# Recurrence of the first layer: products by chunk of 64 tokens and head in the array's four quarters, a PSUM bank to each row half, inverses joined to 64x64 blocks

## The chip, the cores and the metric

The kernel runs on one core of one Trainium2 chip. The metric is the device time in microseconds (us) of one execution, the median over runs. TensorE (PE in the rows; PEld is its weight load) multiplies, VectorE (DVE), ScalarE (ACT) and GpSimd (POOL) work element by element, SyncE (SP) issues the DMAs. Each engine runs its instructions in the order in which the program lists them.

## The reference, cut to what matters

Two residual layers on 512 tokens of width 1024. The first layer's mixer has two halves: sparse attention (8 heads of 64, the best 128 keys by an indexer) and RWKV-7 time mixing (8 heads of 64), a generalised delta rule that the change touches:

```
def step(state, inp):
    r_t, w_t, k_t, v_t, kk_t, a_t = inp
    sa = einsum('bhvk,bhk->bhv', state, -kk_t)
    state = state * w_t + sa[..., None] * (kk_t * a_t) + v_t[..., None] * k_t
    return state, einsum('bhvk,bhk->bhv', state, r_t)
_, y = lax.scan(step, state0, xs)          # 512 tokens, state 64x64 for each of 8 heads
y = head_norm(y) * gn_g + gn_b
y = (y + bonus) * g
```

Then come an output projection, a feed-forward block and a gated embedding; the second layer (mLSTM) and a second feed-forward block follow. All of it is float32.

## The kernel before, in words

Activations lie with features on the 128 partitions and the 512 tokens along the free dimension. `project` makes the large products: each float32 weight is split into a high and a low part, and three matmuls (lines 212 to 214) of 128x128 by 128x512 are added in PSUM. These are most of the program.

The recurrence (`rwkv`) is brought into chunk form. The 512 tokens are eight chunks of 64, handled two at a time: `c` runs over four pairs of 128 tokens, `i` over the two chunks of a pair, which lie on the two row halves of a token-major tile. Heads lie in pairs too: head h = 2j+g is on row half g of feature tile j. For each pair of chunks:

- `r_in` makes the strictly lower products of the keys (`pair_products`, line 719, masked on DVE), turns tiles to token-major (`tokens`, line 833) and makes the right side z = [W | U].
- `corner` (for two pairs at once) builds 32x32 blocks of the inverse of the unit triangular matrices, with the off-diagonal 32x32 block in a tile `off`. `expand` (lines 823 to 827) spreads these on POOL into a 128x128 block-diagonal matrix per head, and `r_apply` (line 916) multiplies it with z.
- `r_read` makes the products of the queries with both keys (`pair_products` again, four calls), and line 928 masks each on DVE and widens it to a 128x128 matrix per head, whose other chunk's block is zero.
- `r_step` makes q (line 944), then for each chunk G and H (bank "gh", lines 958, 960, 963), and carries the state over (line 975, then lines 978 to 980 on DVE). For a chunk G and H are products of rows of one row half.
- `r_out` makes the output y: two products over all 128 rows (lines 1009 and 1011) and one with the state (line 1016), head pair after head pair, then squares, group norm and gate.

A matmul of 64 rows and 64 columns uses one quarter of the array (rows 0-63 or 64-127, columns 0-63 or 64-127). A float32 matmul stands in the trace as two records, each with its weight load.

PSUM has eight banks: four are `aux` (handed out in turn, and taken again only when the engine that reads the bank is done), three are "mm", one is "po". `take` and `give` hand out SBUF slots in turn.

The order of the instructions follows from `merge` in `rwkv`: the part `front(c)` of the next pair of chunks, `back(c-1)` of the last one, the attention (`attend`, then `mixes`, the output projection's first half) and the embedding's projection (`embed`) are generators that are stepped in fixed ratios, one `yield` at a time; the framework's scheduler then shifts instructions a little. So PE's list interleaves the recurrence with attention and with projections.

Of the kernel before, what the change touches and what calls it, by code (L numbers as in the profile page):

```python
# [18 lines left out]
P = 128  # L19
# [30 lines left out]
class Trunk:  # L50
# [43 lines left out]
    def constants(self):  # L94
# [11 lines left out]
        self.mincl = cp.tile([P, P], F32, name="mincl")  # L106
        tri(self.mincl, OP.is_ge)
        nc.gpsimd.memset(self.mincl[0:64, 64:128], 0.0)
        work = self.take()
        tri(work[:, :P], OP.is_gt)  # L110
        self.mstrict = cp.tile([P, 64], F32, name="mstrict")
        for r in (slice(0, 64), slice(64, 128)):
            nc.gpsimd.tensor_copy(self.mstrict[r], work[r, r])
        self.give(work)

        self.mdiag = cp.tile([P, 4], F32, name="mdiag")
        nc.gpsimd.memset(self.mdiag, 0.0)
        for b in range(4):
            nc.gpsimd.memset(self.mdiag[32 * b:32 * b + 32, b:b + 1], 1.0)
# [591 lines left out]
    def pair_products(self, left, right, c, g):  # L711

        ps = self.aux("pair")
        r = slice(64 * g, 64 * g + 64)
        for j in range(4):

            for i in range(2):
                t = slice(P * c + 64 * i, P * c + 64 * i + 64)
                self.nc.tensor.matmul(ps[64 * i:64 * i + 64, tl(j, 64)], left[j][r, t], right[j][r, t],
                                      start=True, stop=True)  # L720
        return ps[:, :256].rearrange("p (j t) -> p j t", t=64)
# [5 lines left out]
    def pairs_ab(self):  # L727

        nc = self.nc
        self.raws = self.takes(NT, "raw")  # L730
        ab = self.dram.tile([P, 32 * 32], F32, name="ab")
        for c, raw in enumerate(self.raws):
            for g in range(2):
                nc.scalar.copy(self.parity(raw, g), self.pair_products(self.Bt, self.KK, c, g))
            r3 = raw.rearrange("s (h t) -> s h t", t=64)
            for b in range(4):
                p0 = b * 32 + c * 8
                nc.sync.dma_start(ab[p0:p0 + 8].rearrange("h (s t) -> s h t", t=32),
                                  r3[32 * b:32 * b + 32, :, 32 * (b % 2):32 * (b % 2) + 32])
        nc.sync.dma_start(self.big[1][:, :1024], ab)  # L740

    def solve(self):
# [21 lines left out]
        self.invs, self.offs = [None, None], [None, None]  # L764
        self.inv, self.off = [None] * NT, [None] * NT
        return last

    def corner(self, two):
# [24 lines left out]
        nc.vector.transpose(dt, inv)  # L793
        yield
# [13 lines left out]
        off = d  # L808
        nc.scalar.mul(off[0:32], ps[0:32], -1.0)
        nc.vector.tensor_scalar(off[64:96], ps[64:96], -1.0, None, op0=OP.mult)  # L810
        self.invs[two], self.offs[two] = inv, off
        for i in range(2):
            c = 2 * two + i
            self.inv[c], self.off[c] = (t[:, tl(i, 256)].rearrange("p (h t) -> p h t", t=32) for t in (inv, off))
        self.give(dt, f, *self.raws[2 * two:2 * two + 2])
        yield

    def expand(self, out, c, g):

        nc = self.nc  # L820
        o4 = out.rearrange("s (h b t) -> s h b t", b=4, t=32)
        h = slice(4 * g, 4 * g + 4)
        nc.gpsimd.tensor_tensor(o4, self.inv[c][:, h].unsqueeze(2).to_broadcast([P, 4, 4, 32]),
                                self.mdiag.unsqueeze(1).unsqueeze(3).to_broadcast([P, 4, 4, 32]), op=OP.mult)
        for b in (0, 2):
            r = slice(32 * b, 32 * b + 32)
            nc.gpsimd.tensor_copy(o4[r, :, b + 1], self.off[c][r, h])
# [50 lines left out]
    def r_in(self, c):  # L878
# [5 lines left out]
        for g in range(2):  # L884
            nc.vector.tensor_tensor(self.parity(ak, g), self.pair_products(self.Kt, self.KK, c, g),
                                    self.mstrict.unsqueeze(1).to_broadcast([P, 4, 64]), op=OP.mult)
            yield
# [19 lines left out]
    def r_apply(self, c):  # L907
        nc, r = self.nc, self.r[c]
        z, tt = r["z"], self.takes(2, "tt")
        r["X"] = self.takes(2)  # L910
        for g in range(2):
# [7 lines left out]
        self.give(*z, *tt)  # L919

    def r_read(self, c):
        r = self.r[c]
        Rt = [self.Rt[:, j] for j in range(4)]
        mask = self.mincl.rearrange("p (b t) -> p b t", t=64).unsqueeze(1).to_broadcast([P, 4, 2, 64])
        for name, left in (("rb", self.Bt), ("rk", self.Kt)):
            r[name] = self.takes(2)
            for g in range(2):
# [3 lines left out]
                yield  # L931
        if c == NT - 1:
            self.give(*self.KK, *self.Bt, *self.Kt, *self.invs, *self.offs)

    def r_step(self, c):
        nc, r = self.nc, self.r[c]
        Bk, Kk, V = r["B"], r["K"], self.V[c]
        head = lambda h: (h // 2, slice(64 * (h % 2), 64 * (h % 2) + 64))
        W, U = self.WU(c)

        ps = self.aux("q")
        for h in range(8):
            j, p = head(h)
            nc.tensor.matmul(ps[p, tl(j)], W(h), r["rb"][h % 2][:, tl(h // 2)], start=True, stop=True)
        r["q"] = q = self.take()
        nc.vector.tensor_tensor(q.rearrange("p (j t) -> p j t", t=P), ps.rearrange("p (j t) -> p j t", t=P),
                                self.Rt[:, :, tl(c)], op=OP.add)
        yield
        r["S"] = [self.state]
        for i in range(2):  # L950
            n = 2 * c + i
            k = slice(64 * i, 64 * i + 64)
            ps = self.aux("gh")
            for j in range(4):
                two = [(h, head(h)[1]) for h in (2 * j, 2 * j + 1)]
                o = slice(256 + 64 * j, 256 + 64 * j + 64)
                for h, p in two:
                    nc.tensor.matmul(ps[p, o], Bk[k, tl(h, 64)], U(h)[k], start=True, stop=False)
                for h, p in two:
                    nc.tensor.matmul(ps[p, o], Kk[k, tl(h, 64)], V[k, tl(h, 64)], start=False, stop=True)  # L960
                if n:
                    for h, p in two:
                        nc.tensor.matmul(ps[p, tl(j, 64)], W(h)[k], Bk[k, tl(h, 64)], start=True, stop=True)
            new = self.take()
            pl = self.PL[:, n].unsqueeze(2).to_broadcast([P, 4, 64])
            s3 = new[:, :256].rearrange("p (j v) -> p j v", v=64)
            if n:
                gh = self.take()
                nc.scalar.copy(gh, ps)
                yield  # L970
                ps = self.aux("step")
                state = self.state
                for h in range(8):
                    j, p = head(h)
                    nc.tensor.matmul(ps[p, tl(j, 64)], gh[p, tl(j, 64)], state[p, tl(j, 64)],
                                     start=True, stop=True)
                sh = gh[:, 256:]
                nc.vector.tensor_tensor(sh, sh, state[:, :256], op=OP.add)
                nc.vector.tensor_tensor(sh, sh, ps[:, :256], op=OP.add)
                nc.vector.tensor_tensor(s3, sh.rearrange("p (j v) -> p j v", v=64), pl, op=OP.mult)  # L980
                self.give(gh)
            else:
                nc.vector.tensor_tensor(s3, ps[:, 256:].rearrange("p (j v) -> p j v", v=64), pl, op=OP.mult)
# [3 lines left out]
        self.give(Bk, Kk)  # L987
# [6 lines left out]
    def r_out(self, c):  # L994
# [3 lines left out]
        rb, rk, q, states = r["rb"], r["rk"], r["q"], r["S"]  # L998
# [5 lines left out]
        ps = self.aux("y")  # L1004

        for j in range(4):
            two = [(h, slice(64 * (h % 2), 64 * (h % 2) + 64)) for h in (2 * j, 2 * j + 1)]
            for h, p in two:
                nc.tensor.matmul(ps[p, tl(j)], U(h), rb[h % 2][:, tl(j)], start=True, stop=False)
            for h, p in two:  # L1010
                nc.tensor.matmul(ps[p, tl(j)], self.V[c][:, tl(h, 64)], rk[h % 2][:, tl(j)], start=False, stop=False)
            for i in range(2):
                k = slice(P * j + 64 * i, P * j + 64 * i + 64)
                for h, p in two:
                    if states[i] is not None:
                        nc.tensor.matmul(ps[p, k], states[i][p, tl(j, 64)], q[p, k], start=False, stop=i == 1)
        y, sq = self.takes(2)
        y3 = y.rearrange("p (j t) -> p j t", t=P)
        nc.scalar.activation(sq, ps, AF.Square)
        nc.vector.tensor_tensor(y3, ps.rearrange("p (j t) -> p j t", t=P), self.gate[:, :, tl(c)], op=OP.mult)  # L1020
# [14 lines left out]
        self.give(y, sq, *rb, *rk, q, *r["X"], self.V[c], *(s for s in states[:2] if s is not None))  # L1035
# [519 lines left out]
```

## Time and profile before

| what | value |
|---|---|
| median of 3 runs | 1625.3 us (1624.97 to 1631.96) |
| the profiled execution, its own time | 1628.07 us |
| its span on the core | 1626.4 us |
| PE busy | 1563.8 us (96% of the span) |
| DVE, ACT, POOL busy | 947.5, 684.6, 311.9 us |

In a row of the busiest groups stands: line, engine, operation, output<-inputs, shapes, number of instructions | busy time (overlaps counted once), mean duration of one in ns | idle time of the engine before them and what ended it. A matmul's duration holds its way through the array, so neighbours overlap: what one costs is read from the distance of the starts. The recurrence lies between 195 and 350 us of the span.

### The profile page before, as it was taken

The page shows a single profiled execution, that of the slowest core. Times are in us where ns is not written, and L with a number is a line of the kernel's source. Part 1 is how long each engine was busy: PE and PEld are TensorE (multiplying, and loading weights), DVE is VectorE, ACT ScalarE, POOL GpSimd, SP SyncE. Part 2 cuts the span into 40 slices and gives each one's busy share as a digit, 9 for nine tenths or more (in the row PEclk, how much of TensorE's full clock was granted, in tenths as well). Part 3 has the DMA queues.
Part 4 walks back from the last instruction along what each step waited for, and adds up shares of the span by engine and source line. Part 5 has one row for each costly group of instructions (what it writes and reads, how often), then busy time and mean ns, then how long its engine had stood idle before and what let it go on. Part 6 is the DMA issues. An engine that isn't in the chain of part 4 may idle for free.

```text
span 1626.4 us, 24626 instructions
## 1 busy us (share of the span) xinstructions
PE 1563.8 (96%) x9446; PEld 1260.8 (78%) x9446; DVE 947.5 (58%) x1755; ACT 684.6 (42%) x1259; POOL 311.9 (19%) x292
## 2 busy tenths in 40 slices
PE   8889899999999999999999999999999999999998
PEld 5566668778888888888777777787778888888887
DVE  6979956666444444335676657566664444443345
ACT  5643465525333333324454555353453333333233
POOL 5545230212000000002400334352430000000002
PEclk9989999999999999999999999999999999999999
DMA  4124120113332333334322113121232333333332
GB/s 165 46 66 132 44 93 2 48 65 95 96 97 94 98 97 110 94 104 139 123 85 85 53 46 104 59 65 62 62 104 91 98 97 98 97 94 96 97 103 98
DMA packets 90110, 142.42 MB, mean 88 GB/s; under 512 B 19588, under 2 KB 24708, under 8 KB 89992
## 3 DMA queue, kind: packets, MB, share of 16 engines
q1 hardware_dynamic: 89992, 140.84, 28.1%
q8 instruction: 74, 1.21, 0.3%
q14 instruction: 44, 0.36, 0.1%
HBM read 133.26 MB, written 7.54 MB: 87 GB/s over the span
## 4 chain that ended last, share of the span: by engine, by line
PE 71%; DVE 6%; issue 1%; ACT 1%; POOL 1%; DMA 0%; DVEq 0%; POOLq 0%
PE mm L212 22%; PE mm L213 21%; PE mm L214 21%; PE v L1296 1%; PE S L1263 1%; PE S L1264 1%; PE num L1310 1%; PE S L1262 1%; PE num L1312 1%; PE num L1311 1%; POOL t L1425 1%; PE gates L1148 1%; DVE wlo L173 0%; DVE t L1342 0%; DVE t L1424 0%
## 5 line engine op out<-in xcount | busy, mean ns | idle before, releaser
L172 ACT CAST whi<-wraw 128x512 fp32r<-128x512 f32 (+1 forms) x470 | 283.9, 606 | 576.7 <-PE mm L213 519.8
L212 PE MATMUL mm<-x,whi 128*128 128x512 f32 (+1 forms) x1248 | 492.0, 394 | 3.3 <-ACT x L298 3.3
L214 PE MATMUL mm<-x,wlo 128*128 128x512 f32 (+1 forms) x1248 | 488.8, 392 | 3.4 <-POOL wlo L173 3.3
L213 PE MATMUL mm<-x,whi 128*128 128x512 f32 (+1 forms) x1248 | 488.3, 391 | 0.3 <-DVE x L299 0.3
L173 DVE TENSOR_TENSOR wlo<-wraw,whi 128x512 fp32r<-128x512 f32 x352 | 244.4, 695 | 247.3 <-ACT whi L172 246.7
L212 PEld LDWEIGHTS mm<-x,whi 128*128 128x128 f32 x1248 | 235.7, 189 | 56.8 <-ACT x L298 3.7
L214 PEld LDWEIGHTS mm<-x,wlo 128*128 128x128 f32 x1248 | 236.0, 189 | 53.7 <-POOL wlo L173 5.1
L213 PEld LDWEIGHTS mm<-x,whi 128*128 128x128 f32 x1248 | 236.0, 189 | 48.5 <-issue 1.2
L173 POOL TENSOR_TENSOR wlo<-wraw,whi 128x512 fp32r<-128x512 f32 (+1 forms) x118 | 154.4, 1314 | 317.1 <-ACT whi L172 309.5
L308 POOL TENSOR_TENSOR t<-t 128x512 f32<-128x512 f32 x42 | 56.7, 1351 | 764.2 <-ACT t L307 763.9
L212 PE MATMUL mm<-h,whi 128*128 128x512 f32 x352 | 136.9, 389 | 0.0
L213 PE MATMUL mm<-h,whi 128*128 128x512 f32 x352 | 136.9, 389 | 0.0
L214 PE MATMUL mm<-h,wlo 128*128 128x512 f32 x352 | 136.9, 389 | 0.0
L214 PEld LDWEIGHTS mm<-h,wlo 128*128 128x128 f32 x352 | 66.1, 188 | 13.8
L213 PEld LDWEIGHTS mm<-h,whi 128*128 128x128 f32 x352 | 66.1, 188 | 13.7
L212 PEld LDWEIGHTS mm<-h,whi 128*128 128x128 f32 x352 | 66.1, 188 | 13.7
L1371 DVE TENSOR_TENSOR t<-mm,t 128x512 f32<-128x512 f32 x44 | 30.4, 692 | 67.1 <-PE mm L214 67.1
L1369 DVE TENSOR_TENSOR t<-mm,t 128x512 f32<-128x512 f32 x44 | 30.4, 692 | 66.4 <-PE mm L214 64.8
L177 ACT CAST h<-t 128x512 fp32r<-128x512 f32 x44 | 27.3, 621 | 65.0 <-DVE t L1372 65.0
L212 PE MATMUL mm<-y,whi 128*128 128x512 f32 x128 | 51.4, 401 | 1.1 <-DVE t L1353 1.1
L213 PE MATMUL mm<-y,whi 128*128 128x512 f32 x128 | 51.5, 402 | 0.0
L214 PE MATMUL mm<-y,wlo 128*128 128x512 f32 x128 | 50.9, 397 | 0.0
(387 smaller groups left out, 2159.1 us busy)
## 6 DMA issues: line engine op xcount, KB each, us to landing
wraw<-in_ffn_w_gate_dram SPq DMA_DIRECT2D x88, 256.0 KB, 2.6
wraw<-in_ffn_w_up_dram SPq DMA_DIRECT2D x88, 256.0 KB, 2.6
wraw<-in_ffn_w_down_dram SPq DMA_DIRECT2D x80, 256.0 KB, 2.7
wraw<-in_c_w_up_dram SPq DMA_DIRECT2D x64, 256.0 KB, 2.6
wraw<-in_w_in_dram SPq DMA_DIRECT2D x38, 256.0 KB, 2.6
wraw<-in_ple_w_gate_dram SPq DMA_DIRECT2D x32, 256.0 KB, 2.7
wraw<-in_c_w_down_dram SPq DMA_DIRECT2D x32, 256.0 KB, 2.6
t<-in_x_dram SPq DMA_DIRECT2D x16, 256.0 KB, 3.0
```

The costliest lines, as they stand in the source:

```text
L172: nc.scalar.copy(hi, raw)
L173: self.wlo_engine.tensor_tensor(lo, raw, hi.bitcast(F32), op=OP.subtract)
L177: self.nc.scalar.copy(hi, src)
L212: nc.tensor.matmul(out, hi[:, c], xh, start=k == 0, stop=False)
L213: nc.tensor.matmul(out, hi[:, c], xl, start=False, stop=False)
L214: nc.tensor.matmul(out, lo[:, c], xh, start=False, stop=k == n - 1)
L308: nc.gpsimd.tensor_tensor(self.acc, self.acc, sq, op=OP.add)
L1148: nc.tensor.matmul(self.gps[32 * c:32 * c + 8, :P], self.maps[:, i, tl(w, 8)], src[:, tl(c)], start=False, stop=i == 15 and w == 1, tile_p ...
L1262: nc.tensor.matmul(ps[:, :n], xhi[i][:, c_], qhi[i][:, o:], start=i == 0, stop=False)
L1263: nc.tensor.matmul(ps[:, :n], xhi[i][:, c_], qlo[i][:, o:], start=False, stop=False)
L1369: nc.vector.tensor_tensor(gt, pg, self.rstd, op=OP.mult)
L1371: nc.vector.tensor_tensor(ut, pu, self.rstd, op=OP.mult)
```

## The change

Five things change, all in the recurrence. `pair_products` makes both heads of a pair in one go, into two banks, one for each row half, and walks through the four quarters of the array in turn; `r_read` makes the products with both keys in one call, and keeps 64x64 blocks where it widened them to 128. G and H of both chunks are made in one go in two banks, ahead of q; q and y go chunk by chunk, a bank to each chunk's row half. The output's state product is cut into pieces of 32 columns. `expand` is gone: `corner` writes the inverses as 64x64 blocks into a tile for each pair of chunks (POOL copies and zeros, then ACT and DVE the corner), and `r_apply` multiplies by quarter.

```
-    def pair_products(self, left, right, c, g):
-        ps = self.aux("pair")
-        r = slice(64 * g, 64 * g + 64)
-        for j in range(4):
-            for i in range(2):
-                t = slice(P * c + 64 * i, P * c + 64 * i + 64)
-                self.nc.tensor.matmul(ps[64 * i:64 * i + 64, tl(j, 64)], left[j][r, t], right[j][r, t],
+    def pair_products(self, lefts, right, c):
+        ps = [self.aux("pair") for _ in range(2)]
+        for l, left in enumerate(lefts):
+            for j in range(4):
+                o = slice(256 * l + 64 * j, 256 * l + 64 * j + 64)
+                for i in range(2):
+                    t = slice(P * c + 64 * i, P * c + 64 * i + 64)
+                    for g in range(2):
+                        r = slice(64 * g, 64 * g + 64)
+                        self.nc.tensor.matmul(ps[g][64 * i:64 * i + 64, o], left[j][r, t], right[j][r, t],
...
     def corner(self, two):
...
         nc.vector.transpose(dt, inv)
+        for i in range(2):
+            self.inv[2 * two + i] = whole = self.take("inv")
+            w4 = whole.rearrange("p (h b t) -> p h b t", h=8, t=32)
+            i4 = inv[:, tl(i, 256)].rearrange("p (h t) -> p h t", t=32)
+            for b in range(4):
+                s = slice(32 * b, 32 * b + 32)
+                nc.gpsimd.tensor_copy(w4[s, :, b % 2], i4[s])
+                if b % 2:
+                    nc.gpsimd.memset(w4[s, :, 0], 0.0)
...
-    def expand(self, out, c, g):
...
     def r_apply(self, c):
-        for g in range(2):
-            self.expand(tt[g], c, g)
...
-                nc.tensor.matmul(ps[:, tl(i)], tt[g][:, tl(i)], z[g][:, tl(i)], start=True, stop=True)
+                for k in (slice(0, 64), slice(64, 128)):
+                    nc.tensor.matmul(ps[k, tl(i)], inv[k, tl(4 * g + i, 64)], z[g][k, tl(i)], start=True, stop=True)
...
     def r_read(self, c):
-        for name, left in (("rb", self.Bt), ("rk", self.Kt)):
-            r[name] = self.takes(2)
-            for g in range(2):
-                self.nc.vector.tensor_tensor(
-                    r[name][g].rearrange("p (j b t) -> p j b t", b=2, t=64),
-                    self.pair_products(left, Rt, c, g).unsqueeze(2).to_broadcast([P, 4, 2, 64]), mask, op=OP.mult)
+        r["rbk"] = self.takes(2)
+        for t, ps in zip(r["rbk"], self.pair_products([self.Bt, self.Kt], Rt, c)):
+            self.nc.vector.tensor_tensor(t.rearrange("p (l j t) -> p l j t", j=4, t=64), ps, mask, op=OP.mult)
...
     def r_step(self, c):
+        ps = [self.aux("gh") for _ in range(2)]
+        each = [(i, k, h) for j in range(4) for i, k in enumerate(chunks) for h in (2 * j, 2 * j + 1)]
+        for n in range(0, 16, 4):
+            for left, right in ((Bk, None), (Kk, V)):
+                for i, k, h in each[n:n + 4]:
+                    j, p = head(h)
+                    nc.tensor.matmul(ps[i][p, 256 + 64 * j:320 + 64 * j], left[k, tl(h, 64)],
+                                     U(h)[k] if right is None else right[k, tl(h, 64)],
...
+        gh = self.takes(2)
+        for i in range(2):
+            o = 0 if c or i else 256
+            nc.scalar.copy(gh[i][:, o:], ps[i][:, o:])
+        yield
...
+        ps = [self.aux("q") for _ in range(2)]
+        for i, k, h in each:
             j, p = head(h)
-            nc.tensor.matmul(ps[p, tl(j)], W(h), r["rb"][h % 2][:, tl(h // 2)], start=True, stop=True)
+            nc.tensor.matmul(ps[i][p, tl(j, 64)], W(h)[k], rbk[h % 2][k, tl(j, 64)], start=True, stop=True)
...
     def r_out(self, c):
-        ps = self.aux("y")
+        ps = [self.aux("y") for _ in range(2)]
+        for l in range(2):
+            for j in range(4):
+                for i, k in enumerate(chunks):
+                    for h in (2 * j, 2 * j + 1):
+                        left = U(h)[k] if l == 0 else self.V[c][k, tl(h, 64)]
+                        nc.tensor.matmul(ps[i][chunks[h % 2], tl(j, 64)], left,
...
+        for i in range(2):
+            for j in range(4):
+                for e in range(2):
+                    for p in chunks:
+                        if state[i]:
+                            v = slice(p.start + 32 * e, p.start + 32 * e + 32)
+                            nc.tensor.matmul(ps[i][v, tl(j, 64)], states[i][p, 64 * j + 32 * e:64 * j + 32 * e + 32],
...
+        for i in range(2):
+            yi = ps[i][:, :256].rearrange("p (j t) -> p j t", t=64)
+            nc.scalar.activation(sq4[:, :, i], yi, AF.Square)
+            nc.vector.tensor_tensor(y4[:, :, i], yi, self.gate[:, :, P * c + 64 * i:P * c + 64 * i + 64], op=OP.mult)
```

In the lists of instructions below, a name is output<-inputs, then the output's shape; lines are those of the kernel listed. On PE, from the first step of the state (L975) of the third pair of chunks (c = 2) on, the kernel before has (s is attention, akv the front of the next pair of chunks):

```order
L975 MATMUL step<-t 64x64 x8
L194 MATMUL s<-k_1391,st 128x512
L194 MATMUL s<-k_1390,st 128x512
L194 MATMUL s<-k_1391,st 128x512
L897 MATMUL akv<-t 64x64 x8
L958 MATMUL gh<-t 64x64 x2
L960 MATMUL gh<-t 64x64 x2
L963 MATMUL gh<-t 64x64 x2
```

and goes on with G and H of the second chunk up to the second step. The changed kernel has, from the first step (now L977) to the second:

```order
L977 MATMUL step<-t 64x64 x8
L188 MATMUL s<-k_1385,st 128x512
L188 MATMUL s<-k_1386,st 128x512
L188 MATMUL s<-k_1385,st 128x512
L188 MATMUL s<-k_1386,st 128x512
L892 MATMUL akv<-t 64x64 x8
L977 MATMUL step<-t 64x64 x8
```

The second chunk's G and H have moved ahead of the first step, so less stands between the two steps. Where the same pair of chunks makes its output y, the kernel before has, after its second step (po is attention, tok the next pair's front):

```order
L693 MATMUL po<-t 64x128 x7
L833 MATMUL tok<-ident,t 128x128 x4
L1009 MATMUL y<-t 64x128 x2
L1011 MATMUL y<-t 64x128 x2
L1016 MATMUL y<-t 64x64 x4
L1009 MATMUL y<-t 64x128 x2
```

and repeats the last three lines for each pair of heads; the changed kernel has:

```order
L892 MATMUL akv<-t 64x64 x8
L1011 MATMUL y<-t 64x64 x32
L1021 MATMUL y<-t 32x64 x32
L687 MATMUL po<-t 64x128 x8
L827 MATMUL tok<-ident,t 128x128 x4
L255 MATMUL sums<-t,hsel 32x128 x4
```

The output no longer changes between two shapes for each pair of heads: 32 products by quarter stand in one stretch, then 32 pieces of 32 columns.

On POOL, around the first inverses, the kernel before has (wlo is the low part of a projection's weights):

```order
L173 TENSOR_TENSOR wlo<-wraw,whi 128x256 x4
L823 TENSOR_TENSOR tt<-inv,mdiag 128x512 x2
L173 TENSOR_TENSOR wlo<-wraw,whi 128x512 x2
L823 TENSOR_TENSOR tt<-inv,mdiag 128x512
L827 COPY tt<-d 32x4x32 x3
L823 TENSOR_TENSOR tt<-inv,mdiag 128x512
L827 COPY tt<-d 32x4x32 x5
```

and the changed kernel:

```order
L167 TENSOR_TENSOR wlo<-wraw,whi 128x256 x4
L799 MEMSET inv 32x8x32 x2
L238 TENSOR_SCALAR rt_h<-rqq 128x32
L799 MEMSET inv 32x8x32 x2
L167 TENSOR_TENSOR wlo<-wraw,whi 128x256 x4
L797 COPY inv<-inv 32x8x32 x8
L167 TENSOR_TENSOR wlo<-wraw,whi 128x512 x3
```

Nothing of POOL stands between the corner blocks and the product any more; eight copies stand in one stretch ahead of the weights' low parts.

## Rows read from the trace of the kernel before

**Rows 1.** The page, busy time of each engine.
```profile
PE 1563.8 (96%) x9446; PEld 1260.8 (78%) x9446; DVE 947.5 (58%) x1755; ACT 684.6 (42%) x1259; POOL 311.9 (19%) x292
```
**Rows 2.** Window 195 to 350 us: length, busy time of each engine, granted clock, DMA.
```profile
195.00:350.00 155.00, 146.47 (x2654) 115.84 (x2653) 95.19 (x277) 81.17 (x224) 29.28 (x43) 0.98 0.15 51
```
**Rows 3.** Waits of PE, 195 to 380 us: total us, times, longest.
```profile
PE apply L916 <- POOL tt L827: 3.4, 2, 2.5
PE mm L212 <- DVE t L1046: 1.9, 1, 1.9
```
**Rows 4.** PE's groups by line, 195 to 350 us.
```profile
L958 PE MATMUL gh<-t 64*64 64x64 f32 x128 | 10.4, 223 | 0.0
L960 PE MATMUL gh<-t 64*64 64x64 f32 x128 | 10.0, 218 | 0.0
L963 PE MATMUL gh<-t 64*64 64x64 f32 x112 | 9.0, 218 | 0.0
L719 PE MATMUL pair<-Rt,t 64*64 64x64 f32 x256 | 8.3, 224 | 0.0
L719 PE MATMUL pair<-t 64*64 64x64 f32 x128 | 6.6, 236 | 0.5 <-DVE t L928 0.5
L789 PE MATMUL half<-d,t 32*32 32x32 f32 x256 | 3.0, 193 | 1.3 <-issue 1.1 <-ACT t L783 0.2
```
**Rows 5.** PE in order of time around 244 us: start us, us, instruction.
```profile
243.96 0.22 PE L958 MATMUL gh<-t 64*64 64x64 f32 x1
243.96 0.22 PE L719 MATMUL pair<-t 64*64 64x64 f32 x1
243.97 0.22 PE L958 MATMUL gh<-t 64*64 64x64 f32 x1
244.02 0.22 PE L719 MATMUL pair<-t 64*64 64x64 f32 x1
244.13 0.28 PE L958 MATMUL gh<-t 64*64 64x64 f32 x4
244.25 0.28 PE L960 MATMUL gh<-t 64*64 64x64 f32 x4
```
**Rows 6.** PE in order of time, third pair of chunks: q, step, y.
```profile
301.46 1.09 PE L944 MATMUL q<-t 128*64 128x128 f32 x16
302.48 0.51 PE L719 MATMUL pair<-t 64*64 64x64 f32 x10
...
305.14 0.68 PE L975 MATMUL step<-t 64*64 64x64 f32 x16
305.75 0.96 PE L194 MATMUL s<-k,st 128*128 128x512 f32 x3
...
310.65 0.68 PE L975 MATMUL step<-t 64*64 64x64 f32 x16
...
312.87 0.44 PE L1009 MATMUL y<-t 128*64 128x128 f32 x4
...
316.73 0.66 PE L833 MATMUL tok<-ident,t 128*128 128x128 f32 x4
```
**Rows 7.** POOL's groups by line and shape, 195 to 350 us.
```profile
L823 POOL TENSOR_TENSOR tt<-inv,mdiag 128x512 f32<-128x512 f32 x8 | 8.3, 1050 | 12.8 <-DVE inv L792 9.3 <-issue 2.1 <-PE apply L916 1.4
L827 POOL COPY tt<-d 32x128 f32<-32x128 f32 x16 | 4.7, 318 | 2.8 <-ACT d L809 1.6 <-DVE d L810 1.0
```
**Rows 8.** DVE's groups by line and shape, 195 to 350 us.
```profile
L928 DVE TENSOR_TENSOR t<-pair,mincl 128x512 f32<-128x512 f32 x16 | 10.4, 684 | 1.1 <-PE pair L719 1.0
L980 DVE TENSOR_TENSOR t<-t,PL 128x256 f32<-128x256 f32 x7 | 4.0, 574 | 0.2
L979 DVE TENSOR_TENSOR t<-t,step 128x256 f32<-128x256 f32 x7 | 2.9, 421 | 1.4 <-PE step L975 1.2
```
**Rows 9.** All engines in order of time, 230 to 235 us.
```profile
230.37 2.95 DVE L670 TENSOR_SCALAR big<-big,rsum 128x256 f32<-128x256 f32 x2
...
234.51 2.05 PE L916 MATMUL apply<-t,tt 128*128 128x128 f32 x16 [2.48 <-POOL tt L827]
```

More of the change, by code (lines that the diff above doesn't have):

```diff
@@ L908, in r_apply @@
         nc, r = self.nc, self.r[c]
-        z, tt = r["z"], self.takes(2, "tt")
+        z, inv = r["z"], self.inv[c]
         r["X"] = self.takes(2)
-        for g in range(2):
-            self.expand(tt[g], c, g)
         for g in range(2):
@@ L938, in r_step @@
         head = lambda h: (h // 2, slice(64 * (h % 2), 64 * (h % 2) + 64))
+        chunks = [slice(0, 64), slice(64, 128)]
         W, U = self.WU(c)
-        ps = self.aux("q")
-        for h in range(8):
-            j, p = head(h)
-            nc.tensor.matmul(ps[p, tl(j)], W(h), r["rb"][h % 2][:, tl(h // 2)], start=True, stop=True)
-        r["q"] = q = self.take()
-        nc.vector.tensor_tensor(q.rearrange("p (j t) -> p j t", t=P), ps.rearrange("p (j t) -> p j t", t=P),
-                                self.Rt[:, :, tl(c)], op=OP.add)
+        ps = [self.aux("gh") for _ in range(2)]
@@ new lines, in r_step @@
+        each = [(i, k, h) for j in range(4) for i, k in enumerate(chunks) for h in (2 * j, 2 * j + 1)]
[5 more added lines that the diff above has]
+                                     U(h)[k] if right is None else right[k, tl(h, 64)],
+                                     start=n == 0 and right is None,
+                                     stop=n == 12 and right is not None and not (c or i))
+            for i, k, h in each[n:n + 4]:
+                j, p = head(h)
+                if c or i:
+                    nc.tensor.matmul(ps[i][p, tl(j, 64)], W(h)[k], Bk[k, tl(h, 64)], start=False, stop=n == 12)
@@ L951, in r_step @@
             n = 2 * c + i
[L952 to L963, printed above, removed]
             new = self.take()
@@ L986, in r_step @@
             yield
-        self.give(Bk, Kk)
+        self.give(Bk, Kk, *gh)
     def WU(self, c):
@@ L997, in r_out @@
         W, U = self.WU(c)
-        rb, rk, q, states = r["rb"], r["rk"], r["q"], r["S"]
+        rbk, q, states = r["rbk"], r["q"], r["S"]
         if c == NT - 1:
@@ L1003, in r_out @@
                 self.split(*(t[:, :P * c] for t in self.yb[j]), self.bonus[:, j, :P * c])
-        ps = self.aux("y")
[L1006 to L1016, printed above, removed]
+        ps = [self.aux("y") for _ in range(2)]
@@ new lines, in r_out @@
+        chunks = [slice(0, 64), slice(64, 128)]
+        state = [x is not None for x in states]
+        for l in range(2):
[4 more added lines that the diff above has]
+                        nc.tensor.matmul(ps[i][chunks[h % 2], tl(j, 64)], left,
+                                         rbk[h % 2][k, 256 * l + 64 * j:256 * l + 64 * j + 64],
+                                         start=l == j == 0, stop=l == 1 and j == 3 and not state[i])
@@ L1034, in r_out @@
                 self.split(*(t[:, tl(c)] for t in self.yb[j]), b3[:, j])
-        self.give(y, sq, *rb, *rk, q, *r["X"], self.V[c], *(s for s in states[:2] if s is not None))
+        self.give(y, sq, *rbk, q, *r["X"], self.V[c], *(s for s in states[:2] if s is not None))
         if c == NT - 1:
```

91 lines of the change are left out of this document (40 added, 51 removed).

## The prediction

> **What bounds the kernel now.** I read the page first: PE is busy for 1563.8 us, 96% of the span, and no other engine reaches 60% [rows 1]. So a change can win only what it takes off PE's list or off PE's waits. Then I looked at the stretch of the recurrence alone, 195 to 350 us [rows 2]: of 155 us PE is busy 146.5, DVE 95.2, ACT 81.2, POOL 29.3, and the granted clock is 0.98, so nearly all of it runs at the upper level, 2.4 GHz. The stage is PE's, with some 8.5 us of idle time in it. The view of PE's waits names the largest piece of that: 3.4 us in two waits of the product with the inverses (L916) for POOL's spreading (L827) [rows 3]. A wait of 1.9 us of a projection for DVE lies behind the recurrence and stays. The third view is PE in order of time: it gives the price of one product as a distance of starts, which a mean duration doesn't (a duration holds the way through the array).
>
> **The price of a product.** Each float32 product of 64x64 by 64 columns is two records. Where PE has only one row half to work on, four records start in 0.12 us: L958 x4 at 244.13, L960 x4 at 244.25 [rows 5], which is 29 ns each, two quarters side by side. At 243.96 and 243.97 the end of a pair product (L719, one row half, one bank) meets the beginning of G and H (L958, the other row half, another bank): two L958 and an L719 start within 0.01 us, and the next L719 at 244.02 [rows 5]. So a row half keeps its own pace of 58 ns for its two quarters while the other works, and all four run at once. Four per 58 ns is 14.5 ns a record. That is the whole basis of the change: a list that goes through the quarters in turn, with two banks, should hold the pace of that short meeting. Each stretch of one shape also pays for its beginning and end: 16 records of step take 0.61 us from 305.14 to 305.75 [rows 6], 0.46 by 29 ns each, so 0.15 us for the switch.
>
> **Part by part, on PE.**
>
> - Pair products in the stage: 256+128 records [rows 4], 29 down to 14.5 ns: 384 x 14.5 ns = 5.6, I take 5.5 us. The same products ahead of the stage (for the solver) I count at nothing: the solver behind them runs on DVE.
> - G and H: 128+128+112 = 368 records [rows 4], at 14.5 ns less 5.3 us; eight stretches become four, which saves 0.6 where they stood alone; some already joined others. I take 5.5.
> - q: 16 records take 1.02 us, 301.46 to 302.48 [rows 6], over all 128 rows with 128 columns, half of them zeros. Now 32 records by quarter: 32 x 14.5 ns + 0.15 = 0.61. Gain 0.41 for each of four pairs of chunks, 1.6 us.
> - y: 3.86 us, 312.87 to 316.73 [rows 6], for 16+16+32 records with eight changes of shape. The first pair of chunks has 16 records less (its first chunk has no state), about 3.4. Together 3.4 + 3 x 3.86 = 15.0. After: 64 records by quarter, 0.93; 64 pieces of 32 columns, which no row shows; two switches, 0.3. The pieces are bounded by the 32x32 products, 256 in 3.0 us or 11.7 ns [rows 4], and by 29 ns; I take 14.5, as four tiles are in use, 0.93 (half for the first pair). Together 8.2 us; gain 6.8, and 3.6 or 7.4 at the bounds.
> - The product with the inverses: 16 records over the whole array become 32 by two quarters on the diagonal, each with 128 columns. q's row gives about 0.11 us for two such at once, 16 x 0.11 = 1.8 us for a pair of chunks, and before it is busy 2.05 us with the way through the array in it [rows 9]. Nothing, give or take 0.3 each.
>
> Sum on PE: 5.5 + 5.5 + 1.6 + 6.8 = 19.4 us.
>
> **POOL.** The spreading goes, 8.3 + 4.7 us [rows 7]. Sixteen copies with 256 elements a partition come, between one and two of the shown copies of 128 (0.32 to 0.64 us), 5 to 10 us, and eight zero fills, which no row shows (0 to 0.6 each). What PE can get back is the 3.4 us of waiting [rows 3]. Against it: while POOL spread, two small DVE operations (L670) took 2.95 us [rows 9], so DVE is held up by POOL's work on SBUF. The changed list has eight copies in one stretch, 2.6 to 5.1 us, ahead of three low parts of weights that PE's projections wait for, and DVE has two L670 there ahead of the transposition that the corner's next product needs. So the wait is partly moved ahead of the corner. I take 1.0 us of gain; the ends are 5 us lost (both corners fully held up) and 3.4 won.
>
> **DVE and ACT.** Sixteen masks of 0.684 us become eight, 5.5 us less on DVE [rows 8]; q, y and the corner are read in two pieces, which gives back under 2 us. Hidden either way beside PE.
>
> **Waits that come.** First, the state: from one step to the next DVE adds and scales, 0.42 + 0.57 = 1.0 us [rows 8]. Between the steps PE had 4.9 us of other work, 305.75 to 310.65 [rows 6]; now four attention products and the eight of akv stand there, about 1.2 + 0.6 = 1.8 us (by 0.96 for three and 0.61 for 16 records). That covers 1.0 us and one DVE operation queued ahead of it, not two. I take 0.3 for each of three pairs, 1.0 together. Second, the banks: of four aux banks each of five products for a pair of chunks (strict keys, queries, G and H, q, y) now takes two at once, 20 times in all. PE, with all its list behind it, waits until ACT or DVE has emptied both. With attention between most of them I take 0.15 each, 3.0; the ends are 0 and one operation of 0.68 each, 14.
>
> By the Trainium skill, page "TensorEngine Tiling (Array Packing)", section "PSUM Bottleneck", tiling speeds up TensorE and not the emptying of PSUM, so that after a speedup the copies may become the bound. Rows 2 speak against that here, with DVE at 61% and ACT at 52% of the stage; if it held, the time would be the first rival's.
>
> **Sum.** 19.4 + 1.0 - 4.0 = 16.4 us. Against the profiled execution's own 1628.07 us that is 1611.7. The median of the runs, 1625.3, lies 2.8 below it, so the forecast is 1609 us. Its own range is 1602 to 1615: waits of 0 to 8, the pieces at their bounds, POOL at 2 lost to 3.4 won.
>
> **Rivals.**
>
> - *The gain is half eaten by emptying banks.* The waits come to some 12 us, 0.6 for each of the 20 groups. Then 19.4 + 1 - 12 = 8.4, about 1617. For it: every group takes half of the banks, and DVE has long operations in line. Against it: rows 2, and that masks leave DVE. 0.15.
> - *A floor under the start of a record.* If starts come no closer than 25 ns, pairs gain 1.5, G and H 1.5, q 0.3, y 15.0 - 13.2 = 1.8, in all 5.1; less 3 for waits and POOL, 2, so 1623. Against it: 256 records in 3.0 us [rows 4] and three starts in 0.01 us [rows 5]. 0.05. The Trainium skill, page "TensorE: Matmul & The Clock Gate", section "Wait — 56ns, not 53.3ns?", states such a floor, about 25 ns however small the product; by that rule the time would be this one, but the trace disagrees for a quartered array, with 11.7 ns.
> - *The change doesn't do what it says.* The meeting in rows 5 is an accident of two products, and in a long stretch the row halves take turns (29 ns). Then PE gains about 1 us, the waits remain: 1626 to 1628 on the median's scale. 0.04.
> - *Slower: PE stands at the banks.* A group finds both banks still to be read, behind one other operation on ACT or DVE: 0.68 + 0.8 = 1.5 us, 20 times, 30 us against the 20.4 won, 1635. It decides from 1.0 us a group on. For it: two groups in a row (G and H, then q) take all four banks. Against it: before, PE hardly waited for an eviction in the stage; the waits on POOL and DVE of rows 3 are larger. 0.05.
> - *More than the sum*: no wait comes, POOL's wait goes, and the products ahead of the stage count too: 19.4 + 3.4 + 2 = 25, 1600. 0.05.
>
> **The numbers.** The forecast has 0.66. About 0.5% (8 us) is what a measurement of this kernel can tell from no change. Faster than 1617: the forecast, the last rival and half of the first, 0.78. Within 0.5%: the other half, the floor, and no effect, 0.17. Slower: 0.05. A range from 1600 to 1620 leaves out the floor, no effect, the banks and a little at each end of the others, some 0.2.
>
> **What would show it.** In the profile after: starts of the pair products, of G and H, q and the first part of y at four per 58 ns, in stretches of 64 to 96 records in 1.0 to 1.5 us; y of a pair of chunks in 2.2 us; no wait of the product with the inverses for POOL, or one moved to the corner; PE's waits for a bank or for the state under 0.5 us each, about 4 us together; the stage some 16 us shorter and the rest of the span as before. Wrong it would be if records in these stretches start 25 to 29 ns apart, if PE's idle time in the stage grows by more than 8 us, or if the tail behind 350 us changes by more than 3.

## The result and the profile after

The changed kernel takes 1613.1 us as the median of four runs (1612.3 to 1613.4), beside 1625.2 us for four runs of the kernel before on the same chip. The ratio is 0.9915, with a 95% interval from 0.9889 to 0.9941. So it is faster, by 12.1 us on the medians, where 16 were forecast. The profiled executions lie 14.9 us apart (1613.2 and 1628.1), because that of before lay 2.8 us above the median of its runs.

The first line of the page after, and the window of the stage, answer to [rows 1, 2]. The columns of the second are length, busy time of PE, PE's weight loads, DVE, ACT and POOL, granted clock, DMA share and GB/s.

```profile
PE 1544.3 (96%) x9814; PEld 1246.6 (77%) x9814; DVE 942.2 (58%) x1757; ACT 685.2 (43%) x1266; POOL 307.9 (19%) x288
```
```profile
195.00:350.00 155.00, 141.71 (x3040) 112.56 (x3032) 99.25 (x308) 85.53 (x238) 27.34 (x45) 0.98 0.18 57
```

PE has 368 records more and 19.5 us less to do. A group's busy time also holds the way through the array, so I compare sums of the distance from each start on PE to the next, between one projection ahead of the stage and one behind it (at 194.80 and 390.03 us before, at 193.29 and 374.73 after). They are added up from the trace, in us:

```
           before  after  difference
y           14.99   8.72   -6.27
G and H     11.62   6.71   -4.91
pair        12.69   8.76   -3.93
q            4.96   2.71   -2.25
apply        7.66   7.90   +0.24
idle        11.47  13.29   +1.82
all others 131.84 133.36   +1.52
sum        195.23 181.45  -13.78
```

The four lists (y, G and H, pair products, q) give 17.4 us. Idle time takes 1.8 back, although the wait for POOL [rows 3] is gone. Here are PE's waits in the stage after (total us, times, longest); "issue" means that nothing in the profile's events holds PE. The first line, at 347 us, answers to the 1.9 us of L1046 [rows 3].

```profile
PE mm L206 <- DVE t L1056: 2.4, 1, 2.4
PE sums L255 <- ACT t L595: 2.1, 1, 2.1
PE half L778 <- issue: 1.5, 1, 1.5
PE s L188 <- DVE mx L654: 1.4, 1, 1.4
PE po L687 <- DVE ya L172: 1.2, 1, 1.2
PE q L959 <- issue: 1.0, 1, 1.0
PE half L786 <- issue: 0.9, 1, 0.9
PE step L977 <- DVE t L981: 0.6, 2, 0.3
PE mm L207 <- DVE ya L172: 0.5, 1, 0.5
PE y L1021 <- issue: 0.4, 1, 0.4
PE mm L206 <- ACT pe L1413: 0.4, 1, 0.4
PE pt L677 <- ACT t L678: 0.2, 1, 0.2
PE apply L910 <- ACT inv L818: 0.2, 1, 0.2
```

The pace is seen in PE's order of time inside a list of G and H (L941, L948) of the second pair of chunks, the place that answers to [rows 5]:

```profile
259.25 0.39 PE L941 MATMUL gh<-t 64*64 64x64 f32 x12
259.43 0.22 PE L948 MATMUL gh<-t 64*64 64x64 f32 x1
259.47 0.23 PE L941 MATMUL gh<-t 64*64 64x64 f32 x3
259.49 0.27 PE L948 MATMUL gh<-t 64*64 64x64 f32 x4
259.55 0.22 PE L941 MATMUL gh<-t 64*64 64x64 f32 x1
259.59 0.23 PE L948 MATMUL gh<-t 64*64 64x64 f32 x3
259.61 0.39 PE L941 MATMUL gh<-t 64*64 64x64 f32 x12
```

From 259.25 to 259.61 there are 24 starts, 15.0 ns each. y of the third pair, which took 3.86 us [rows 6], now takes 2.72, a wait included:

```profile
301.24 1.10 PE L1011 MATMUL y<-t 64*64 64x64 f32 x62
302.28 0.64 PE L1021 MATMUL y<-t 64*32 64x64 f32 x31
303.37 0.66 PE L1021 MATMUL y<-t 64*32 64x64 f32 x33 [0.45 <-issue]
303.96 1.09 PE L687 MATMUL po<-t 128*64 128x128 f32 x16
```

### The profile page after: what moved, and what is told of

Its sections match the earlier page's. It is cut to its first block, busy times and chain, and to the rows that moved or that the text cites. A ratio compares the mean times of both kernels' runs of the same rounds, so it can differ in the third digit from the quotient of the medians.

```text
span 1611.3 us, 25367 instructions
## 1 busy us (share of the span) xinstructions
PE 1544.3 (96%) x9814; PEld 1246.6 (77%) x9814; DVE 942.2 (58%) x1757; ACT 685.2 (43%) x1266; POOL 307.9 (19%) x288
## 4 chain that ended last, share of the span: by engine, by line
PE 72%; DVE 6%; ACT 1%; issue 1%; POOL 1%; DMA 0%; DVEq 0%; POOLq 0%
PE mm L206 22%; PE mm L207 21%; PE mm L208 21%; PE v L1306 1%; PE num L1320 1%; PE S L1273 1%; PE num L1321 1%; PE S L1274 1%; PE num L1322 1%; PE S L1272 1%; POOL t L1435 1%; PE gates L1158 1%; DVE wlo L167 1%; PE spread L274 0%; DVE t L1352 0%
## 5 line engine op out<-in xcount | busy, mean ns | idle before, releaser
L207 PEld LDWEIGHTS mm<-h,whi 128*128 128x128 f32 x352 | 66.1, 188 | 13.8
L208 PEld LDWEIGHTS mm<-h,wlo 128*128 128x128 f32 x352 | 66.1, 188 | 13.7
```

What stands on the lines that cost most here:

```text
L207: nc.tensor.matmul(out, hi[:, c], xl, start=False, stop=False)
L208: nc.tensor.matmul(out, lo[:, c], xh, start=False, stop=k == n - 1)
```

## The experiments

The theory: the gain is PE's time in the four lists, because four quarters work at once, less some waits. The rivals: POOL's part or the shapes carry the change; the new waits are for banks; part of the difference is chance. "The stage" below is the stretch of the table above.

**Row halves in turn.** Each list is walked one row half after the other.

```
-    for l ... for j ... for i ... for g in range(2):   # pair products
+    for g in range(2): for l ... for j ... for i ...
-each = [(i, k, h) for j in range(4) for i, k in enumerate(chunks) for h in (2*j, 2*j+1)]
+each = [(i, k, h) for i, k in enumerate(chunks) for h in range(8)]
```


> The changed kernel with its banks, its masks, its joined inverses and its shapes, but each list walked one row half after the other (pair products, G and H, q, both parts of y), so that only two quarters work at a time. Theory (the gain is quarters at work side by side): the lists go back to 29 ns a record. Pair products 8.8 to 12.7 us, G and H 6.7 to 11.6, q 2.7 to 3.9, y 8.7 to 14, and 1.9 to 2.8 ahead of the stage: 16 to 18 us longer, 1629 to 1631. Rival (the gain is POOL's spreading gone and fewer changes of shape, both of which stay here): at most 3 us longer, 1613 to 1616.

Measured 1620.3 us, 0.9947 of before [0.9928, 0.9966]; the changed kernel itself did not run on that chip, and the nearest to it is the third experiment's, 1612.6. The stage is 188.5 us long, 7.1 more than after. The y of the third pair shows the pace, with its parts from L1011 and L1021:

```profile
300.42 1.86 PE L1011 MATMUL y<-t 64*64 64x64 f32 x63
302.21 1.79 PE L1021 MATMUL y<-t 64*32 64x64 f32 x64
303.93 1.09 PE L687 MATMUL po<-t 128*64 128x128 f32 x16
```

It is 28 and 27 ns a record now. The lists cost 11.4 us more than in the changed kernel (pair 11.5, G and H 10.1, q 3.4, y 13.3), so quarters side by side are worth 11.4 of the 17.4 us. The other 6.0 stay with row halves too. What is left of the change in these lists is longer stretches of one shape and, in q, no zeros; no run takes the two apart. I had priced none of that when I expected 16 to 18. And of the 11.4 only 7.1 show, since PE's idle time fell by 2.8 (and all other work by 1.5): the slower lists hide waits that the quick ones meet. Which waits, the later runs tell.

**The joined inverses alone.** The kernel before with the new `corner` and `r_apply`.

> The kernel before with one part of the change alone: inverses joined to 64x64 blocks and the product with them by quarters, so POOL's spreading is gone and the sixteen copies come. Theory: the 3.4 us that PE waited for POOL go, up to 2.4 come back at the corner: 1.0 to 3.4 us faster than before, 1622 to 1624. Rival (POOL's part carries the change): 8 us or more faster, 1617 or less. Second rival (the copies hold up both corners): up to 5 slower, 1630.

Measured 1630.0 us, 1.0012 of before [0.9991, 1.0033]: no gain. The stage is 195.3 us long, like before's 195.2. Its waits:

```profile
PE half L788 <- issue: 3.3, 2, 1.9
PE sums L261 <- ACT t L601: 1.8, 1, 1.8
PE sums L268 <- ACT rows L267: 0.7, 1, 0.7
PE apply L911 <- ACT ya L177: 0.6, 1, 0.6
```

The 3.4 us for POOL are gone, but the corner's second list waits 3.3 where it waited 1.1, and pair products and apply are 1.4 us longer. (Both waits of `half` end 1.3 and 1.6 us behind the landing of a load of code; what that means is shown below.) POOL's part carries nothing of the change: the first rival falls, and so does my 1.0 to 3.4. The second, up to 5 us slower, is not excluded by the interval (1.5 us faster to 5.4 slower on 1627.4). Its mechanism is not seen, since both waits are behind code; but this stage was at the lower clock, 1.2 GHz, for 3.4 us only and that of before for 10.2, so its equal length may hide a small loss.

**The solver's products by row halves.** Only `pairs_ab` gets the old walk.

> The changed kernel, with the 128 records of pair products for the solver, ahead of the stage, walked row half by row half as before; all else as changed. In the two traces PE passes these products 2.8 us sooner after the change (1.3 late at 105 us, 1.5 early at 115), and the granted clock there was 0.5 before and 1.0 after. Theory A (shorter list, and the clock stays up because of it): 2.8 us longer, 1616, with the clock at 0.5 in 107 to 113 us. Theory B (the list alone): 1.0 to 1.9 longer, 1614 to 1615, clock at 1.0. Theory C (hidden beside the solver, as the prediction had it; what the traces show is chance): within 0.5 of the changed kernel.

Measured 1612.6 us, 0.9909 [0.9882, 0.9937], not slower than the changed kernel, and the clock stays up at 107 to 113 us, so theory A falls. The interval, some 4 us to either side, can't tell B from C. The trace can: the stage begins at 192.9 us, at 193.3 and 193.2 in the two traces of the changed kernel, with 13.7 us at the lower clock ahead of it in all three. That speaks for C: the list is hidden. Where the stage begins goes with the time at the lower clock before it: from 188.9 us with 3.4 us of it (the next experiment) to 196.9 with 23.9 (the joined inverses alone).

**G and H chunk by chunk.** Behind q, as before, in one bank each.

```
+    for i in range(2):
+        ps = self.aux("gh")      # one chunk, one row half, just ahead of its step
```


> The changed kernel with G and H again made for one chunk at a time, in one bank, just ahead of that chunk's step and behind q, as before the change; pair products, q, y and the inverses stay as changed. Theory: G and H go from 6.7 back to 11.6 us, and some 1 us of waits (step for the state 0.6, q for a bank) goes: 3 to 4.5 us longer, 1616 to 1618. Rival (G and H ahead of q bring the new waits, 2 banks at once twice in a row and the state chain bare, and cost what they gain): 1611 to 1613, with PE's waits in the stage some 4 us less.

Measured 1619.7 us, 0.9954 [0.9938, 0.9971]. In the stage G and H are back at 11.6 us, q costs 3.7, and idle time is 0.8 more, not less: 5.9 us longer in all. That is more than the 3 to 4.5 expected, because q became dearer too and idle time did not fall: q now waits 2.0 us for the masks that it reads (DVE L921), a wait that the changed kernel, with G and H between them, does not have. The making of G and H together pays in full, and it is not the source of the waits.

**The changed kernel again.**

> The changed kernel itself, on the chip and beside the runs of the next kernels, and to see how far one profile of it differs from another. Theory (the gain is the four lists of the recurrence, 17 us of PE's time in the first trace, less about 4 us of waits and of longer neighbours): faster than before by 12 to 15 us, and the four lists within 0.5 us of the first trace (pair 8.8, G and H 6.7, q 2.7, y 8.7). Rival (a part of the 13.8 us by which the stage shrank is the luck of where the clock fell): 8 to 11 us, with other stretches at the lower level.

Measured 1612.0 us beside 1625.6 of before, 0.9916 [0.9901, 0.9931], 13.6 us apart. The lists agree (pair 8.76, G and H 6.71, q 2.71, y 8.51). The stage is 179.4 us against 181.5. In it the granted clock was at the lower level for 6.8 us (from 197) against 10.2 (from 201, 276 and 351). So one trace of a kernel against another is good to about 2 us. The 13.8 us of the first comparison are not luck of the clock within the stage: before and after were both at the lower level for 10.2 us there.

**Five banks for the recurrence, two for the rest.**

```
-banks(c, 3, 4)
+banks(c, 2, 5)
```


> The changed kernel with five aux banks and two for projections and attention, in place of four and three. Theory (the new waits of PE in the stage come from two aux banks being taken at once): PE's idle time in the stage falls by 2 to 4 us where recurrence products wait, and if projections and attention can do with two banks, 1 to 3 us faster than the changed kernel. Rival (the waits are for attention's and the norms' own chains on DVE and ACT, not for banks): no gain; scores and projections wait for a bank more often, 3 us slower or worse.

Measured 1614.2 us, 0.9928 [0.9913, 0.9943]. The waits of the corner stay, and scores and norms wait longer:

```profile
PE sums L255 <- ACT t L595: 4.0, 1, 4.0
PE pt L677 <- DVE mx L654: 2.0, 3, 1.1
PE half L778 <- issue: 1.5, 1, 1.5
PE half L786 <- issue: 1.4, 1, 1.4
PE step L977 <- DVE t L981: 0.6, 2, 0.3
```

So a fifth bank wins nothing, and no wait of the recurrence shrinks: the theory of banks falls for the changed kernel. The trial isn't clean, since it takes a bank from attention, and its stage was at the lower clock for 17.1 us.

**What the "issue" waits are.** Every one at `half` (the corner's first two lists), q and y ends shortly after a 16 KB packet on the DMA queue of kind "instruction". This is that queue in a window of 1.3 us of the changed kernel (packets, MB, share), and PE in order of time around it, where the corner's list stops after 118 of 128 records:

```profile
q8 instruction: 1, 0.02, 5.9%
```
```profile
272.92 1.20 PE L778 MATMUL half<-invt,raw 16*32 16x32 f32 x118
275.60 0.30 PE L778 MATMUL half<-invt,raw 16*32 16x32 f32 x10 [1.47 <-issue]
```

Read from the trace's DMA packets and PE's records (us):

```
kernel  PE waits at   from    to      load starts  lands   go-on after landing  records since start
before  half L789    220.93  222.04   219.32      220.69   1.35                 112
after   half L786    218.62  219.47   216.60      218.06   1.41                 114
after   q    L959    260.63  261.64   259.23      260.17   1.47                  81
after   half L778    274.12  275.60   272.97      274.20   1.40                 114
after   y    L1021   302.92  303.37   301.05      302.02   1.35                 101
row     half L786    216.25  216.87   214.56      215.67   1.20                 113
halves
```

PE uses up its instructions before more come. The stage after has 25 such loads, one to some 127 records, and from the start of a load PE goes on 2.3 to 2.9 us later. The places say the same. Counted in PE's records from the start of the stage, the stops after lie at 406, 1299, 1681 and 2446, which is 406 plus 7, 10 and 16 times 127.5. All 43 "issue" waits over 0.15 us in the stages of the fourteen traces lie on this grid to within 3 records, once the 64 put in by one run below are counted; that of before lies at 406 too. By these rows, as an estimate, a list longer than a load covers can't average much under 2.4 us / 127 = 19 ns a record; the closest two loads in any of the traces start 3.3 us apart, 26 ns a record. Some loads begin late (20 records before the stop at q in the run with 64 more records, below), and what sets their start no run shows. The waits of this kind come to 1.1 us before, 3.8 after, and 0.6 with row halves, about the idle time that the first experiment won back.

**Attention begun two pieces later.**

```
-merge(front(0), (at, 1.2), (em, 0.6))
+merge(front(0), (at, 1.3), (em, 0.6), due=[-2.0, 0.0])
```


> The changed kernel with attention begun two pieces later in the first pair of chunks, and then at 1.3 pieces instead of 1.2. In the changed kernel's trace PE stands 2.1 us for the squares of the queries and 1.4 for the first row maximum at 195 to 201 us, and the granted clock falls behind it. Theory (PE's waits that are left belong to the start of attention, and the clock dip hangs on them): both waits go, 2 to 5 us faster than the changed kernel. Rival (the work that is put in their place then lacks at a later place, or DVE is late anyway): within 1 us.

Measured 1610.3 us (1608.9 to 1611.9), 0.9904 [0.9887, 0.992], beside 1612.0 for the changed kernel on that chip. The 2.1 and 1.4 us are gone, 1.6 appear in their place, and the clock fell at 202 us all the same. That the clock hangs on these two waits is not borne out. It is the fastest version seen, by 1.7 us, less than the intervals separate.

**Attention spread thinner.** The rates 1.0, 0.6 and 0.7 for 1.2, 0.7 and 0.8.

> The changed kernel with attention spread thinner over the recurrence: 1.0, 0.6 and 0.7 pieces for one of the recurrence in place of 1.2, 0.7 and 0.8. Theory (the recurrence's shorter lists bring attention's pieces closer together, so that scores and values wait for DVE, 1.4 and 1.2 us in the changed kernel's trace): these waits go, 1 to 3 us faster. Rival (attention covers the recurrence's own chain, and what is left of it ends the stage later): 0 to 4 us slower.

Measured 1614.3 us, 0.9938 [0.9914, 0.9962]; idle time in the stage grew to 16.0 us, with 1.8 for scores and 1.0 for values still in it. The theory falls. The runs spread from 1609.2 to 1626.8 us, too far to show the 2.3 us as a loss; the idle time speaks for the rival, that attention is the cover.

**Loads moved by 64 records.** Two groups of the solver's products are issued twice.

```
+    for c in range(2):
+        self.pair_products([self.Bt], self.KK, c)
```


> The changed kernel with 64 more records of pair products in the solver's list ahead of the stage, whose results nothing reads; the stage's list is as changed. In the traces PE's waits in the middle of a list of small products (the corner's 1.5 and 1.3 us, q 0.7 to 1.0, y 0.4) end 1.2 to 1.6 us behind the landing of a 16 KB load on the instruction queue, with 81 to 117 records issued since the load began. Theory (PE has run out of instructions: a list that goes faster than its code comes): the loads fall 64 records earlier in the lists, so these waits change place and size; those in the second corner at 274 to 280 us go below 0.5 and others appear. Rival (they are waits for a bank, for DVE or for ACT): the same waits at the same places. Time either way within 2 us of the changed kernel.

Measured 1616.8 us, 0.9933 [0.991, 0.9955], with a stage of 179.9 us. The waits in the second corner are gone, and q waits instead, 1.54 us behind the landing of another load:

```profile
292.64 0.62 PE L961 MATMUL q<-t 64*64 64x64 f32 x25
295.12 0.33 PE L961 MATMUL q<-t 64*64 64x64 f32 x4 [1.86 <-issue]
```
```profile
PE q L961 <- issue: 1.9, 1, 1.9
PE spread L274 <- DVE t L270: 1.3, 1, 1.3
PE po L687 <- DVE ya L172: 1.2, 1, 1.2
PE half L788 <- issue: 1.0, 1, 1.0
```

Nothing in the stage's work, banks or tiles was changed, only where the loads fall. The stops are now at records 343, 1491, 1874, 2128 and 2256 of the stage: the same grid of 127.5, moved ahead by the 64 records put in. That shows the theory of code. Its time is 3.7 us above the next run's on the same chip, more than the 2 expected; the changed kernel did not run on that chip.

**The corner's lists in halves**, and that with attention later.

```
             # both lists of corner, behind the products of n
+            if n == 7:
+                yield
```


> The changed kernel with each of the corner's first two lists of 128 small products given in two halves, and attention's or a projection's pieces set between them; two empty places behind the masks are taken out in turn. Theory (code): the longer instructions between give the load its time, the waits of the corner's first products, 2.4 to 4.2 us in the changed kernel's two traces, fall below 1 us, and the kernel is 1 to 4 us faster. Rival (bank, DVE or ACT): the waits stay, and so does the time.

> The changed kernel with both edits: attention begun two pieces later, and the corner's first lists in halves. Theory: their gains add, 1610.3 less 1 to 3 us, 1607 to 1609. Rival (what one saves the other had saved already, or the clock falls elsewhere): 1609 to 1611.

Measured 1613.1 us, 0.9909 [0.9884, 0.9935], and 1616.5 us, 0.9929 [0.9903, 0.9956]. The corner's waits fell to 1.3 us in the first, from 2.3 and 4.2 in the two traces of the changed kernel, not below the 1 expected, and no time was won: q and y now wait 1.2 each behind a load, and G and H 2.2 for masks on DVE. The gains of the two edits do not add.

**A piece of attention inside the lists.** One between G and H and q, one between the two parts of y.

> The changed kernel with attention begun two pieces later, and with one piece of attention set between G and H and q and one between the two parts of y; 0.6 and 0.7 pieces elsewhere in place of 0.7 and 0.8. Theory (code): where longer instructions now part the lists (y in all pairs, G and H from q in the first), no wait behind a 16 KB load is left there (0.4 to 0.7 us at y in the changed kernel and in that with attention begun later); where pair products, G and H and q still run on as one list of some 200 records (second and third pair) it stays or grows, 0.5 to 1.9. Together within 2 us of 1610.3. Rival (those are waits for DVE, ACT or a bank): waits of y stay at 0.4 to 0.7.

Measured 1619.5 us, 0.9937 [0.9916, 0.9958]. No y waits behind a load any more, as the theory of code wants it; the 0.5 to 1.9 expected in the lists that still run on did not come either. But G and H wait 3.5 us for masks:

```profile
PE gh L941 <- DVE t L921: 3.5, 2, 2.1
```

G and H read no mask's output. In the trace two groups of pair products stand just ahead (those of the queries and of the keys, at 255 to 257 us), which take all four banks, and G and H go on when the first of these masks is done. So here, with the lists moved together, banks do cost. The same wait stands at 1.7 to 2.2 us in both runs with the corner's lists in halves and in that with attention spread thinner. The stage is as long as in the second trace of the changed kernel, 179.4 us; behind it a norm waits 3.9 us and the clock falls, which no one edit explains.

## Why the prediction was right, and where its terms were off

The mechanism was right: four quarters with two banks keep the pace of the short meeting in [rows 5], 14.6 to 15 ns in uncut lists, and the floor of 25 ns is not there. The size was 12.1 us on the medians (13.6 when the same kernel ran again) for 16. By terms:

- *PE, 19.4 forecast, 17.1 measured* (the four lists less 0.2 at the apply). Pair products gave 3.9 for 5.5, because attention cuts eight lists into a dozen stretches, and the beginnings and ends cost: in the mean a record takes 22.8 ns, in an uncut list of 64 it is 17 (1.09 us). G and H gave 4.9 for 5.5, q 2.3 for 1.6, y 6.3 for 6.8. The pieces of 32 columns cost 17.3 ns (3.87 us for 224), for 14.5 taken between 11.7 and 29.
- *POOL, +1.0 forecast.* In the changed kernel the wait at the product with the inverses shrank from 3.4 to 0.2 us, as hoped, but alone the joined inverses won nothing. So no run shows the 1.0. The copies and zero fills lie inside their bounds (5 to 10, and 0 to 4.8), 6.4 and 2.4 us in two groups of POOL's:

```profile
L797 POOL COPY inv<-inv 32x256 f32<-32x256 f32 x16 | 6.4, 402 | 7.4 <-DVE inv L789 6.7
L799 POOL MEMSET inv<- 32x256 f32 x8 | 2.4, 304 | 7.1 <-PE s L188 4.3 <-ACT ya L171 2.5
```

- *New waits, 4.0 forecast* (state 1.0, banks 3.0). The state costs 0.6. The recurrence's banks show no wait of their own in the changed kernel. In their place stand instructions that come late (2.7 us more than before) and attention's and the norm's own chains (s 1.4, po 1.2, sums 0.4 more); some waits of before went. Without POOL's 3.2 the idle time grew by 5.0. The size was nearly right by luck, and the cause was wrong: I weighed only what a semaphore can show.
- *Net.* 16.4 forecast on the profiled executions' scale, 14.9 measured. The stage gave 13.8: 2.3 us less on PE, 1.5 for longer neighbours that I had not counted, and idle time 1.2 better than the 3.0 of POOL and new waits together. Another 1.5 came ahead of the stage, where the trace of before was at the lower clock for 20.5 us and that of after for 13.7. As far as the traces show that is chance: with the changed list the clock fell at 106 us too, in the run with both edits above. 0.4 was lost elsewhere. On the medians the gain is smaller still, 12.1: I took the 2.8 us that before's profiled execution lay above its median for a constant, and after's lay on its median. Why is open, but for the 1.5.
- *The range.* Its upper end, 1615, doesn't follow from its own bounds: waits of 8, the pieces at 29 ns (3.2 less) and POOL at 2 lost leave 6.2 us, which is 1619. 1613.1 lies inside either way.
- *What it said would show it.* Lists of 92 and 96 records took 1.34 and 1.40 us, within the 1.0 to 1.5 forecast; y of a full pair of chunks took 2.1 to 2.7 us, for 2.2; the stage was 13.8 shorter for some 16; idle time grew by less than 8; the tail stayed within 3.
- *Rivals.* That the row halves take turns is refuted by the first experiment; whether one bank would do for both was not tried. Banks as the slower case did not come; nor did "half eaten by emptying banks" (new waits of about 5 us, for another cause, where 12 were assumed). The Trainium skill's floor, page "TensorE: Matmul & The Clock Gate", section "Wait — 56ns, not 53.3ns?", is refuted for a quartered array by the 15.0 ns above.

## What to carry to other kernels

Price small products by the distance of their starts, and spread them over all four quarters with a bank to each row half: it took 11 us off PE here, and the rest of the change in these lists, longer stretches of one shape above all, another 6. Then count records as code too: here a list of some hundred records under 20 ns each outran its own instructions at the end of what had been loaded, and part of the gain comes back as waits that no semaphore explains. Look for such waits beside the instruction queue's packets before blaming a bank.

## What the hardware showed that was not expected

- *Code comes at a pace.* A 16 KB load takes 0.9 to 1.8 us and PE goes on 1.2 to 1.6 us behind its landing. The Trainium skill, page "Runtime: NRT & Kernel Launch", section "Instruction fetch mechanics", calls the crossing of such a block "mostly hidden"; for lists at 11 to 17 ns the traces disagree, with 0.2 to 1.9 us a time.
- *The clock.* At about 195 to 205 us the granted clock is at the lower of its levels, 1.2 GHz, for part of the time in all traces (a mean of 0.58 in 200 to 204 us after), also with attention begun later, where 3.5 us of waits just ahead became 1.6. Behind the 2.4 us wait at 347 us it fell in one execution of the changed kernel (0.50 in 351 to 354 us) and not in another (1.00), though PE waited equally long in both. With a fall at 276 us, likewise in one alone, that goes with the 2 us between their stages.
